# Assembling the 64-block inverses of two heads together, alternating in the array's groups

## The chip, the cores and the metric

The kernel runs on one core of a Trainium2 chip. The metric is the device time of one execution in microseconds; the median of three executions before the change is 1605.24 us (1601.2 to 1608.65). The core has five engines with queues of their own: TensorE (PE, whose weight loads the profile lists as PEld), VectorE (DVE), ScalarE (ACT), GpSimd (POOL) and SyncE (SP, which issues most of the transfers). TensorE's array is 128 x 128; a matmul with at most 32 rows and 32 columns of weights can be placed in one 32 x 32 tile of it (`tile_position=(row, column)`), and then reads operands from the partitions of its rows and writes PSUM partitions of its columns.

## The reference

One layer of a hybrid decoder on 512 prompt tokens and 32 sample tokens (8 sequences of 4): RMSNorm, one input projection, three parallel mixers that read it (RWKV-7 time mixing with 16 heads of 64, sparse attention with an indexer, cross-attention into 256 memory tokens), a gate on each, and an output projection with a final RMSNorm. The change touches the RWKV-7 part alone. Its recurrence over tokens, for each head, is

```python
def step(S, inp):
    r_t, k_t, v_t, w_t, kk_t, a_t = inp
    sa = jnp.einsum('bhvk,bhk->bhv', S, -kk_t)
    S = (S * w_t[:, :, None, :] + sa[..., None] * (kk_t * a_t)[:, :, None, :]
         + v_t[..., None] * k_t[:, :, None, :])
    return S, jnp.einsum('bhvk,bhk->bhv', S, r_t)
```

The kernel does not step through the tokens. It works on chunks of 64: inside a chunk the values `sa` solve a triangular system of 64 equations, whose matrix depends on the keys alone. So the inverse T of each chunk's matrix is made ahead, for all chunks at once, and then a loop over the 8 chunks carries the state.

## The kernel before, in words

After the norm the kernel runs the projections that attention needs, attention itself, and then `rwkv_group(g, ...)` for g = 0 to 3. One call, a head group, holds four heads: `j` (0, 1) is the pair, `h` (0, 1) the head in it, and a head's rows lie on partitions 64h to 64h + 63. Weights of every dense projection come as `raw` tiles of 128 x 512 by SP's queue, are split by ACT into a high part (L341, `wh`) and by DVE into the rest (L344, `wl`), and enter three float32r matmuls with 272 columns for each half of the tokens.

The order of the work is not written by hand. A planner takes every instruction with a priority and issues on each engine what is ready by its own estimate, the smaller number first; the kernel sets the priorities by `level(...)`. Matmuls of dense projections have level "fill", those of RWKV the normal one, so a dense matmul is issued where no RWKV matmul is ready. The projections for the next head group (`ahead("k")`, `ahead("v")`, `ahead("r")`) and the gates are the dense work beside a head group. On the chip each engine then executes its queue in the order planned.

Inside `rwkv_group`:

- L1198 to L1273: decays, keys and the products of keys in each chunk. `MBT` holds for each head and chunk the 64 x 64 matrix of products, of which the block from the first 32 tokens to the last 32 is used below.
- L1292 to L1298: DVE solves all 32 x 32 diagonal blocks of the triangular matrices together (64 blocks on 128 partitions), 31 steps of two operations.
- L1300 to L1302 and L1365 to L1373: the solved blocks go by DRAM (`vd`) into `TT`, the tile with T: partitions 64h + 32b hold the diagonal block b of head h. Two loads serve each head, the two of head 0 first.
- L1377 to L1393, the assembly: the block beside the diagonal is a product of three 32 x 32 matrices, for 16 (pair, chunk) combinations of each h. The loop over h takes one head after the other. DVE transposes the first diagonal block (L1381, one operation for each pair), 16 matmuls multiply it with the block of `MBT` (step 1, L1384), one ACT copy moves the 512 columns from PSUM (L1386), 16 matmuls multiply with the second diagonal block (step 2, L1389), and two ACT copies put the result into `TT` (L1392). Head h works in tile (64h, 64h + 32) of the array in step 1 and in (64h + 32, 64h) in step 2. Each step of each head has a PSUM bank of its own, from a ring of three (`"sc"` and `"tp"` share it).
- L1406 to L1470, `sample()`: the 32 sample tokens, in pieces between the chunks; its first matmuls are 64 x 64 with 8 columns.
- L1486 to L1534: the loop over the 8 chunks. Its products `p1` (L1500) don't need T; `pa` (L1512) does, four matmuls into one bank, `for j` outside and `for h` inside.

All matmuls of RWKV go through `mm`, so the profile gives them line 222, transposes by PE line 228. The tiles that lie in `slots` and `late` are told apart only by these names.

Of the kernel before, what the change touches and what calls it, by code (L numbers as in the profile page):

```python
# [124 lines left out]
def emit(ctx, tc, A):  # L125
    nc = tc.nc
    P = 128
# [14 lines left out]
    def R(shape, dt=F32, name="R", hot=False):  # L142
        n = math.prod(shape[1:]) * (2 if dt == BF16 else 4) // 4
        k = -(-n // SLOT)
        if k > 1:

            i = max((range(j, j + k) for j in range(0, NSLOT, k) if set(range(j, j + k)) <= set(free)),
                    key=lambda r: min(map(free.index, r)))
            for j in i:
                free.remove(j)  # L150
        else:
            i = (free.pop(-1 if hot else 0),)
        o = i[0] % 4 * SLOT
        t = quads[i[0] // 4][:shape[0], o:o + n]
        if dt != F32:
            t = t.bitcast(dt)
        if len(shape) > 2:
            ax = ["abcdefg"[d] for d in range(len(shape) - 1)]
            t = t.rearrange("p (%s) -> p %s" % (" ".join(ax), " ".join(ax)),
                            **{a: shape[d + 1] for d, a in enumerate(ax)})  # L160
        held[id(t)] = (i, t)
        return t

    def F(*ts):
        for t in ts:
            if isinstance(t, list):
                F(*t)
            else:
                free.extend(held.pop(id(t))[0])

    def S(shape, dt=F32, tag=None, bufs=None, name=None):
        return spool.tile(shape, dt, tag=tag, name=name or tag, bufs=bufs)

    def PS(shape, tag, dt=F32):
        tag, bufs = {"acc": ("acc", 3), "tp": ("ts", 3), "sc": ("ts", 3)}.get(tag, (tag, 1))
        return ppool.tile(shape, dt, tag=tag, name="ps_" + tag, bufs=bufs)

    act, dve, pool, pe = nc.scalar, nc.vector, nc.gpsimd, nc.tensor
# [5 lines left out]
    @contextmanager  # L184
    def level(n):
        old, tc.cur_priority = tc.cur_priority, levels[n]
        yield
        levels[n], tc.cur_priority = tc.cur_priority, old
# [31 lines left out]
    def mm(out, lhsT, rhs, start=True, stop=True, **kw):  # L220
        with level("fill") if in_side[0] else nullcontext():
            return pe.matmul(out, lhsT=lhsT, rhs=rhs, start=start, stop=stop, **kw)  # L222
# [115 lines left out]
    def split_w(raw, m):  # L338
        wh = wpool.tile([P, KG, P], F32R, tag="wh", name="wh", bufs=3)
        wl = wpool.tile([P, KG, P], F32R, tag="wl", name="wl", bufs=3)  # L340
        splits.append(act.activation(wh[:, :, :m], raw[:, :, :m], AF.Copy))  # L341
        lo_ctr[0] += 1
        eng = pool if lo_ctr[1] and lo_ctr[0] % lo_ctr[1] == 0 else dve
        eng.tensor_tensor(wl[:, :, :m], raw[:, :, :m], wh[:, :, :m].bitcast(F32), op=OP.subtract)  # L344
        return wh, wl
# [54 lines left out]
    for k in range(KO):  # L400
        raw = wpool.tile([P, KG, P], F32, tag="raw", name="raw", bufs=4)
        with level("top"):
# [3 lines left out]
            w = [flat2(t) for t in split_w(raw, P)]  # L406
# [22 lines left out]
    ok_, _ = VROWS["k_a"]  # L429
# [548 lines left out]
    for j in range(4):  # L978
        din(COL["va"] + j * P,
            lambda h, t0, t1, acc, j=j: act.activation(VT[j // 2][:, j % 2, t0:t1], acc[:, :t1 - t0], AF.Copy))  # L980
# [153 lines left out]
    for j in range(4):  # L1134
        din(COL["qm"] + j * P,
            lambda h, t0, t1, acc, j=j: act.activation(QM[j // 2][:, j % 2, t0:t1], acc[:, :t1 - t0], AF.Copy))
# [43 lines left out]
    def rwkv_group(g, pending, XK, XV, XR):  # L1180
# [3 lines left out]
        def ahead(nm, hot=False):  # L1184
            if g < 3:
                with level("late"):
                    nxt.append(rwkv_proj(g + 1, nm, hot))
# [10 lines left out]
        for j in range(2):  # L1198
# [4 lines left out]
            w = W2A2[:, j * P:(j + 1) * P]  # L1203
# [20 lines left out]
            for t0, t1_ in HV:  # L1224
                ps = PS([P, 512], "sc")
# [20 lines left out]
        MBT = R([P, 2, NCH, 64], name="mbt")  # L1246
        md = dpool.tile([64, 1024], F32, name="md", bufs=2)
        mds = dpool.tile([32, 16], F32, name="mds", bufs=2)
        for h in range(2):
            for j in range(2):  # L1250
                for q in range(2):
                    n0 = q * 4
                    ps = PS([P, 4, P], "sc")
# [14 lines left out]
        for h in range(2):  # L1268
            ps = PS([P, 512], "sc")
# [10 lines left out]
        for j in range(2):  # L1280
            dve.scalar_tensor_tensor(RK[:, j], XR[:, j], vec("r_k", 2 * g + j), XK[:, j], op0=OP.mult, op1=OP.mult)
            for (t0, t1), tag in zip(HV, "Lc"):
                ps = PS([P, 512], tag)
# [8 lines left out]
        for s_ in range(31):  # L1292
            i, w = s_ + 1, 31 - s_
            r = (i + 1) // 2
            t = S([P, 136], tag="tb", bufs=1)[:, :r * w].rearrange("p (i w) -> p i w", i=r)
# [18 lines left out]
        for s_ in range(3):  # L1314
            i, w = s_ + 1, 3 - s_
            t = S([32, 4], tag="tbs", bufs=1)[:, :i * w].rearrange("p (i w) -> p i w", i=i)
# [18 lines left out]
        for w in range(2):  # L1335
            p = PS([P, 2, 2, P], "tp")
# [9 lines left out]
        for j in range(2):  # L1346
            p = PS([P, 512], "tp")
# [7 lines left out]
        for j in range(2):  # L1355
            BKT.append(R([P, NCH, P], name="bkt", hot=j > 0))
            for q in range(2):
                p = PS([P, 512], "tp")
# [6 lines left out]
        TT = R([P, 2, NCH, 64], name="tt")  # L1365
        WG = R([P, 2, 512], name="wg")
# [7 lines left out]
        F(MB, VB, XV)  # L1374
        ahead("v")
        ahead("r")
        for h in range(2):  # L1377
            r0, r1 = 64 * h, 64 * h + 32
            w1 = WG[r0:r0 + 32, 0].rearrange("p (i t) -> p i t", t=32)
            for j in range(2):  # L1380
                dve.transpose(w1[:, j * 8:(j + 1) * 8], TT[r0:r0 + 32, j, :, 0:32])  # L1381
            ps = PS([P, 512], "sc")
            for i in range(16):
                mm(ps[r1:r1 + 32, i * 32:(i + 1) * 32], MBT[r0:r0 + 32, i // 8, i % 8, 32:64], w1[:, i],  # L1384
                   tile_position=(r0, r1))
            act.copy(WG[r1:r1 + 32, 1], ps[r1:r1 + 32])  # L1386
            ps = PS([P, 512], "sc")
            for i in range(16):
                mm(ps[r0:r0 + 32, i * 32:(i + 1) * 32], WG[r1:r1 + 32, 1, i * 32:(i + 1) * 32],  # L1389
                   TT[r1:r1 + 32, i // 8, i % 8, 32:64], tile_position=(r1, r0))  # L1390
            for j in range(2):
                act.copy(TT[r0:r0 + 32, j, :, 32:64],  # L1392
                         ps[r0:r0 + 32, j * 256:(j + 1) * 256].rearrange("p (n t) -> p n t", t=32))  # L1393
        F(WG, MBT)

        s0 = R([P, 2, NB, 64], name="smp")
# [88 lines left out]
        for n in range(NCH):  # L1485
            w, i = n // 4, n % 4  # L1486
# [10 lines left out]
            for u in range(2):  # L1497
                for j in range(2):
                    for h in range(2):
                        ins = mm(p1[HS[u], j, h], LB[j][h][:, c0 + 64 * u:c0 + 64 * u + 64], SV[w][:, i, j, h],  # L1500
                                 tile_position=(0, 64 * u))
# [20 lines left out]
            if n < NCH - 1:  # L1522
                w1, i1 = (n + 1) // 4, (n + 1) % 4
# [51 lines left out]
    for g in range(4):  # L1575
        pending, pr = rwkv_group(g, pending, *pr)
# [11 lines left out]
    for i in (4, 5, 6, 7, 0, 1, 2, 3):  # L1588
        if i not in YG:
            gated(i)  # L1590
        t, y = YT[i // 2][:, i % 2 * 2:i % 2 * 2 + 2], YG[i]
# [95 lines left out]
    for g in range(4):  # L1687
# [3 lines left out]
        for n, k in enumerate(KORD):  # L1691
# [3 lines left out]
            with level("fill"):  # L1695
# [5 lines left out]
                if n % 4 == 3:  # L1701

                    for j, (k, raw) in enumerate(raws):
                        mm(accs[4][32 * j:32 * j + 32], YS[:, k], raw, start=n == 3, stop=n == KO - 1,
                           tile_position=(0, 32 * j), skip_group_check=True)
# [74 lines left out]
```

## Time and profile before

| | before |
|---|---|
| median of 3 runs | 1605.24 us (1601.2 to 1608.65) |
| profiled execution | 1605.69 us, its span 1603.9 us |
| PE busy | 1517.4 us, 95% of the span |
| DVE busy | 946.7 us, 59% |
| ACT busy | 679.0 us, 42% |
| POOL busy | 309.2 us, 19% |
| mean granted TensorE clock | 0.98 of full speed |

The span goes from the first to the last instruction of the profiled execution. A busy PE is one with a matmul under way; matmuls overlap, so the busy time of a group is not the sum of its durations. Idle time of an engine is listed with what ended it. In timelines a line merges instructions of one kind that follow each other: the time of the first start, the time from there to the last end, and their number.

### The profile page before, as it was taken

What the parts mean: (1) busy time and instruction counts of PE and PEld (TensorE: products, weight loads), DVE (VectorE), ACT (ScalarE), POOL (GpSimd) and SP (SyncE); (2) the same over time, 40 slices, a digit from 0 to 9 for tenths busy, and PEclk for the clock granted to TensorE, in tenths of its full rate; (3) what the DMA queues carried; (4) which work ended last, traced back from release to release, by engine and by line L of the source; (5) the groups of instructions that cost most, each with busy time, mean ns of one, the idle gap of its engine ahead of it and who ended that gap; (6) DMA issues with size and microseconds to landing.
All of it is one profiled execution on the core that took longest, in us unless ns stands there. A gap on an engine that the chain in (4) does not pass through costs nothing.

```text
span 1603.9 us, 31129 instructions
## 1 busy us (share of the span) xinstructions
PE 1517.4 (95%) x11855; PEld 1292.9 (81%) x11855; DVE 946.7 (59%) x2697; ACT 679.0 (42%) x1482; POOL 309.2 (19%) x463
## 2 busy tenths in 40 slices
PE   8899999889989889889999999999999998999997
PEld 7799955889878875568898898799889988977775
DVE  5846677988565642115864893598368746623233
ACT  7656643222224423225633563465355444522223
POOL 0010121210454544320103011201310023001110
PEclk9999999999989999799999999999999999999999
DMA  7633232322697774456341243225123745472223
GB/s 279 201 109 80 73 113 60 94 69 72 208 292 222 226 213 127 125 173 195 95 113 48 59 115 72 57 60 150 45 57 91 188 145 160 147 232 79 92 93 138
DMA packets 227893, 207.12 MB, mean 129 GB/s; under 512 B 44768, under 2 KB 183200, under 8 KB 227232
## 3 DMA queue, kind: packets, MB, share of 16 engines
q1 hardware_dynamic: 214048, 158.99, 34.3%
q0 software_dynamic: 13696, 46.15, 9.2%
q8 instruction: 93, 1.52, 0.4%
q14 instruction: 56, 0.46, 0.1%
HBM read 180.89 MB, written 24.19 MB: 128 GB/s over the span
## 4 chain that ended last, share of the span: by engine, by line
PE 60%; issue 16%; DVE 11%; ACT 4%; DMA 4%; POOL 3%; another core or an unknown queue 1%; SPq 0%; POOLq 0%; DVEq 0%; ACTq 0%
PE ps_acc L222 31%; PE ps_ts L222 14%; PE ps_c L222 7%; PE ps_L L222 5%; DVE wl L344 2%; PE ps_ts L228 2%; POOL sw L477 2%; DMA late<-qd 1%; DVE slots L1150 1%; ACT wh L341 1%; DMA slots<-qd 1%; POOL wl L344 1%; DVE slots L904 1%; DVE late L785 1%
## 5 line engine op out<-in xcount | busy, mean ns | idle before, releaser
L222 PE MATMUL ps_acc<-xt,wh 128*128 128x272 f32 (+1 forms) x4224 | 862.7, 296 | 6.4 <-ACT lc L442 4.1
L222 PEld LDWEIGHTS ps_acc<-xt,wh 128*128 128x128 f32 (+1 forms) x4224 | 681.8, 190 | 30.1 <-issue 12.3
L222 PE MATMUL ps_acc<-xt,wl 128*128 128x272 f32 (+1 forms) x2112 | 625.4, 296 | 0.0
L222 PEld LDWEIGHTS ps_acc<-xt,wl 128*128 128x128 f32 (+1 forms) x2112 | 402.4, 191 | 9.0 <-issue 2.2
L341 ACT ACTIVATE wh<-raw 128x512 fp32r<-128x512 f32 (+1 forms) x296 | 185.1, 626 | 308.9 <-PE ps_acc L222 261.7
L344 DVE TENSOR_TENSOR wl<-raw,wh 128x512 fp32r<-128x512 f32 (+1 forms) x285 | 196.1, 691 | 133.6 <-ACT wh L341 117.6
L1684 DVE TENSOR_TENSOR wl<-raw,wh 128x512 fp32r<-128x512 f32 x58 | 42.8, 741 | 108.2 <-ACT wh L1683 99.8
L1683 ACT ACTIVATE wh<-raw 128x512 fp32r<-128x512 f32 x58 | 36.3, 630 | 115.4 <-PE ps_c L222 104.3
L222 PE MATMUL ps_acc<-wh,yt 128*128 128x512 f32 x192 | 61.5, 401 | 0.1
L222 PE MATMUL ps_ts<-wh,yt 128*128 128x512 f32 x156 | 50.3, 402 | 0.0
L477 POOL TENSOR_TENSOR sw<-sw,slots 128x272 f32<-128x272 f32 (+1 forms) x18 | 13.9, 773 | 185.2 <-ACT sw L475 185.2
L222 PEld LDWEIGHTS ps_acc<-wh,yt 128*128 128x128 f32 x192 | 35.4, 188 | 13.8 <-ACT wh L1683 5.9
L887 POOL DMA_INDIRECT slots<-ck,gix x36 | 37.4, 1040 | 38.0 <-DVE slots L904 24.0
L887 POOL DMA_INDIRECT slots<-cv,gix x32 | 30.5, 955 | 50.4 <-PE ps_L L222 28.5
L222 PEld LDWEIGHTS ps_ts<-wh,yt 128*128 128x128 f32 x156 | 28.7, 188 | 12.1 <-ACT wh L1683 5.0
L222 PE MATMUL ps_L<-late,slots 32*32 32x512 f32 (+3 forms) x192 | 38.3, 550 | 0.2 <-DMA late<-cmv 0.2
L222 PE MATMUL ps_ts<-slots,slots 64*64 64x512 f32 (+6 forms) x250 | 37.3, 322 | 0.2 <-DVE slots L1381 0.2
L222 PE MATMUL ps_acc<-wl,yt 128*128 128x512 f32 x96 | 37.4, 390 | 0.0
L887 POOL DMA_INDIRECT late<-cv,gix x32 | 30.3, 946 | 32.8 <-PE ps_L L222 23.5
L222 PE MATMUL ps_c<-wh,yt 128*128 128x512 f32 x116 | 36.5, 396 | 0.0
L544 DVE SCALAR_TENSOR_TENSOR slots<-tm,wtm,slots 128x256 f32<-128x256 f32 (+2 forms) x45 | 29.3, 656 | 10.3 <-ACT tm L540 9.7
L439 DVE SCALAR_TENSOR_TENSOR slots<-ps_acc,vecs,slots 128x271 f32<-128x271 f32 (+2 forms) x72 | 26.6, 397 | 13.6 <-ACT slots L438 12.7
(552 smaller groups left out, 2547.6 us busy)
## 6 DMA issues: line engine op xcount, KB each, us to landing
raw<-w_in SPq DMA_DIRECT2D x260, 256.0 KB
raw<-w_out SPq DMA_DIRECT2D x64, 256.0 KB
slots<-xT SPq DMA_DIRECT2D x4, 1088.0 KB
raw<-w_mk SPq DMA_DIRECT2D x16, 256.0 KB
raw<-w_mem SPq DMA_DIRECT2D x16, 256.0 KB
slots<-qd POOLq DMA_DIRECT2D x8, 512.0 KB
late<-qd POOLq DMA_DIRECT2D x8, 512.0 KB
slots<-xp SPq DMA_DIRECT2D x8, 512.0 KB
```

The costliest lines, as they stand in the source:

```text
L222: return pe.matmul(out, lhsT=lhsT, rhs=rhs, start=start, stop=stop, **kw)
L228: return pe.transpose(out, in_, T["ident"][b:b + k, b:b + k])
L341: splits.append(act.activation(wh[:, :, :m], raw[:, :, :m], AF.Copy))
L344: eng.tensor_tensor(wl[:, :, :m], raw[:, :, :m], wh[:, :, :m].bitcast(F32), op=OP.subtract)
L439: add = lambda o, prev: dve.scalar_tensor_tensor(o, prev, mu, o, op0=OP.mult, op1=OP.add)
L477: pool.tensor_tensor(sw[:np_], sw[:np_], sin[:np_, t0:t1], op=OP.mult)
L544: dve.scalar_tensor_tensor(SCP[i], rl[:, :nk], WTM[:, i, hd:hd + 1], SCP[i], op0=OP.mult, op1=OP.add)
L785: dve.tensor_scalar(oa[:, :, a], val[:, 1, sl].rearrange("p (n q) -> p n q", q=4), a, None, op0=OP.is_equal)
L887: pool.indirect_dma_start(out=dst[:, u], out_offset=None, in_=src, in_offset=bass.IndirectOffsetOnAxis(ap=GIX[:, 2 * q + u:2 * q + u + 1], ...
L904: ins = dve.scalar_tensor_tensor(kg[:, u, c], kg[:, u, c], 1.0, qb[:, c], op0=OP.mult, op1=OP.mult, accum_out=SCA[:, u, h, q:q + 1])
L1683: act.activation(wh, raw, AF.Copy)
L1684: dve.tensor_tensor(wl, raw, wh.bitcast(F32), op=OP.subtract)
```

## The change

The loop over h goes. The transposes of both heads come first, then all 32 matmuls of step 1, head 0 and head 1 in turn, into one PSUM bank, then a copy for each head, ACT for head 0 and DVE for head 1, then step 2 in the same way. The second copies take 512 columns in one operation where there were two of 256. The matmuls, their operands and the tiles of the array are the same; two PSUM banks are taken in each head group instead of four. The loads of `TT` and all that stands around are as before.

```diff
         F(MB, VB, XV)
         ahead("v")
         ahead("r")
-        for h in range(2):
-            r0, r1 = 64 * h, 64 * h + 32
-            w1 = WG[r0:r0 + 32, 0].rearrange("p (i t) -> p i t", t=32)
-            for j in range(2):
-                dve.transpose(w1[:, j * 8:(j + 1) * 8], TT[r0:r0 + 32, j, :, 0:32])
-            ps = PS([P, 512], "sc")
-            for i in range(16):
-                mm(ps[r1:r1 + 32, i * 32:(i + 1) * 32], MBT[r0:r0 + 32, i // 8, i % 8, 32:64], w1[:, i],
-                   tile_position=(r0, r1))
-            act.copy(WG[r1:r1 + 32, 1], ps[r1:r1 + 32])
-            ps = PS([P, 512], "sc")
-            for i in range(16):
-                mm(ps[r0:r0 + 32, i * 32:(i + 1) * 32], WG[r1:r1 + 32, 1, i * 32:(i + 1) * 32],
-                   TT[r1:r1 + 32, i // 8, i % 8, 32:64], tile_position=(r1, r0))
-            for j in range(2):
-                act.copy(TT[r0:r0 + 32, j, :, 32:64],
-                         ps[r0:r0 + 32, j * 256:(j + 1) * 256].rearrange("p (n t) -> p n t", t=32))
+        rows = [(slice(64 * h, 64 * h + 32), slice(64 * h + 32, 64 * h + 64)) for h in range(2)]
+        w1 = [WG[q0, 0].rearrange("p (i t) -> p i t", t=32) for q0, _ in rows]
+        for j in range(2):
+            for (q0, _), w in zip(rows, w1):
+                dve.transpose(w[:, j * 8:(j + 1) * 8], TT[q0, j, :, 0:32])
+        ps = PS([P, 512], "sc")
+        for i in range(16):
+            for (q0, q1), w in zip(rows, w1):
+                mm(ps[q1, i * 32:(i + 1) * 32], MBT[q0, i // 8, i % 8, 32:64], w[:, i],
+                   tile_position=(q0.start, q1.start))
+        for (_, q1), f in zip(rows, (act.copy, dve.tensor_copy)):
+            f(WG[q1, 1], ps[q1])
+        ps = PS([P, 512], "sc")
+        for i in range(16):
+            for q0, q1 in rows:
+                mm(ps[q0, i * 32:(i + 1) * 32], WG[q1, 1, i * 32:(i + 1) * 32], TT[q1, i // 8, i % 8, 32:64],
+                   tile_position=(q1.start, q0.start))
+        for (q0, _), f in zip(rows, (act.copy, dve.tensor_copy)):
+            f(TT[q0, :, :, 32:64], ps[q0].rearrange("p (j n t) -> p j n t", j=2, t=32))
         F(WG, MBT)
```

## Rows read from the trace of the kernel before

**Rows 1.** The page, parts 1 and 2: busy time of the engines, and TensorE's granted clock in 40 equal slices of the span, in tenths of full speed.

```profile
PE 1517.4 (95%) x11855; PEld 1292.9 (81%) x11855; DVE 946.7 (59%) x2697; ACT 679.0 (42%) x1482; POOL 309.2 (19%) x463
...
PEclk9999999999989999799999999999999999999999
```

**Rows 2.** The table of stretches for 820 to 880, 940 to 1000, 1120 to 1180 and 1240 to 1300 us, which hold the assemblies of head groups 0 to 3: its line of sums.

```profile
sum 240.00, PE 237.98 PEld 210.31 DVE 118.23 ACT 94.59 POOL 44.26; mean PE 59.50 PEld 52.58 DVE 29.56 ACT 23.65 POOL 11.06
```

**Rows 3.** What PE waited for from 800 to 1300 us: us in total, times, longest.

```profile
PE ps_ts L222 <- DVE late L1381: 0.7, 1, 0.7
PE ps_c L222 <- issue: 0.6, 1, 0.6
...
PE ps_ts L222 <- DVE slots L1381: 0.2, 1, 0.2
```

**Rows 4.** The timeline of PE in the assembly of head group 0: start, us from there to the last end, engine, line, operation, tiles, tile of the array, shape, number. 128x272 is dense work.

```profile
828.53 0.66 PE L222 MATMUL ps_ts<-slots,late 32*32 32x32 f32 x16
...
829.57 0.69 PE L222 MATMUL ps_ts<-slots,late 32*32 32x32 f32 x16
...
831.41 0.41 PE L222 MATMUL ps_acc<-xt,wh 128*128 128x272 f32 x2
831.75 1.19 PE L222 MATMUL ps_ts<-late,slots 32*32 32x32 f32 x32
832.87 0.39 PE L222 MATMUL ps_acc<-xt,wl 128*128 128x272 f32 x1
833.10 0.41 PE L222 MATMUL ps_acc<-xt,wh 128*128 128x272 f32 x2
...
833.57 0.33 PE L222 MATMUL ps_c<-bs,late 64*64 64x64 f32 x2
...
837.78 1.19 PE L222 MATMUL ps_ts<-late,slots 32*32 32x32 f32 x32
838.90 1.10 PE L222 MATMUL ps_ts<-slots,late 64*64 64x8 f32 x32
```

**Rows 5.** The timeline of the weight loads (PEld), two places with loads 64 columns wide: `p1` of chunk 1, four loads for one tile of the array, and `pa` of chunk 1, eight loads whose matmuls alternate between the tiles (0, 0) and (64, 64) and write one PSUM bank.

```profile
844.36 0.31 PEld L222 LDWEIGHTS ps_c<-slots,slots 128*64 128x64 f32 x4
...
846.89 0.31 PEld L222 LDWEIGHTS ps_c<-bs,late 64*64 64x64 f32 x8
```

**Rows 6.** The same view in an earlier stage (sample attention): the first and the last of four lines of weight loads, 32 columns wide, for four column tiles in turn.

```profile
415.53 0.11 PEld L222 LDWEIGHTS ps_ts<-late 128*32 128x32 f32 x2 [0.21 <-DVE keepbias L824]
...
415.57 0.12 PEld L222 LDWEIGHTS ps_ts<-late,slots 128*32 128x32 f32 x2
```

**Rows 7.** The groups of instructions by form, PE: the bf16 matmuls with 32 columns; number, busy us, mean ns of one, idle before.

```profile
L222 PE MATMUL ps_L<-slots,late 128*128 128x32 bf16 x256 | 6.8, 177 | 0.9 <-DVE late L785 0.8
```

**Rows 8.** The timeline of PE in head groups 1 and 2, at the first `pa` matmul, and what DVE waited for from 820 to 1350 us at its copy behind ACT's from the same bank (us, times, longest).

```profile
978.84 0.32 PE L222 MATMUL ps_c<-bs,slots 64*64 64x64 f32 x2
...
1126.13 0.33 PE L222 MATMUL ps_c<-bs,slots 64*64 64x64 f32 x2
...
DVE bs L1506 <- ACT bs L1505: 23.4, 17, 1.9
```

**Rows 9.** The timeline of DVE at the transposes of the assembly: for each head group the line of head 0 and the line of head 1; in brackets DVE's idle time before and what ended it.

```profile
827.96 0.75 DVE L1381 STREAM_TRANSPOSE slots<-late 32x256 f32<-32x256 f32 x2
...
833.13 0.76 DVE L1381 STREAM_TRANSPOSE slots<-late 32x256 f32<-32x256 f32 x2 [0.42 <-DMA late<-vd]
...
973.04 0.76 DVE L1381 STREAM_TRANSPOSE late<-slots 32x256 f32<-32x256 f32 x2 [0.27 <-DMA slots<-vd]
...
979.88 0.76 DVE L1381 STREAM_TRANSPOSE late<-slots 32x256 f32<-32x256 f32 x2
...
1120.51 0.76 DVE L1381 STREAM_TRANSPOSE slots<-slots 32x256 f32<-32x256 f32 x2
...
1125.30 0.76 DVE L1381 STREAM_TRANSPOSE slots<-slots 32x256 f32<-32x256 f32 x2
...
1278.90 0.43 DVE L1381 STREAM_TRANSPOSE late<-slots 32x256 f32<-32x256 f32 x1 [1.48 <-DMA slots<-vd]
...
1281.18 0.76 DVE L1381 STREAM_TRANSPOSE late<-slots 32x256 f32<-32x256 f32 x2 [0.92 <-DMA slots<-vd]
```

**Rows 10.** The views of single lines: number, shortest/median/longest ns of one, first and last start, shape.

```profile
L1386 ACT COPY slots<-ps_ts x4: 577/578/580, 830.3 to 1129.5; 32x512 f32<-32x512 f32 x4
...
L1392 ACT COPY slots<-ps_ts x12: 357/360/363, 978.2 to 1289.7; 32x256 f32<-32x256 f32 x12
...
L1260 DVE TENSOR_TENSOR late<-ps_ts,cmain x14: 693/694/696, 911.3 to 1231.6; 64x512 f32<-64x512 f32 x14
```

**Rows 11.** The table of stretches behind the assemblies of head groups 1 and 2 (us of the stretch; busy us and instructions of PE, PEld, DVE, ACT and POOL; granted clock; DMA share; GB/s), and the timeline of PE in it.

```profile
984.00:988.00 4.00, 4.00 (x65) 3.23 (x62) 0.39 (x2) 0.63 (x2) 1.04 (x1) 0.68 0.23 63
988.00:992.00 4.00, 4.00 (x22) 3.38 (x23) 0.70 (x3) 0.70 (x3) 1.31 (x4) 0.50 0.00 0
...
1134.00:1138.00 4.00, 4.00 (x21) 3.19 (x22) 0.41 (x2) 0.53 (x2) 0.00 (x0) 0.50 0.16 46
...
988.12 0.43 PE L222 MATMUL ps_acc<-xt,wl 128*128 128x272 f32 x1
988.35 0.65 PE L222 MATMUL ps_acc<-xt,wh 128*128 128x272 f32 x2
988.80 0.43 PE L222 MATMUL ps_acc<-xt,wl 128*128 128x272 f32 x1
```

## The prediction

> **What bounds the kernel now.** I read the page first: TensorE (PE) is busy for 95% of the span at a granted clock of 9 tenths or more in nearly every slice [rows 1]. An average over stages says little about one stage, so next the table of stretches: over the four stretches of 60 us that hold the four assemblies PE is busy for 237.98 of 240 us [rows 2], and in all of 800 to 1300 us it waited 0.9 us for the transposes that feed the assembly and 0.6 us for nothing visible [rows 3]. So the dense projections of the next head group fill every gap between the small matmuls, and the price of the assembly is not its chain of waits but the PE time that it takes from the dense work. The reader is to see that in the timeline of the first assembly [rows 4]: dense matmuls (128x272), a block of 32x32 ones, dense ones again, without holes.
>
> From rows 4 come the two prices. (a) Each float32 matmul leaves two records; a head has 16 + 16 + 32 of them, so a head group has 128 and the kernel 512. A block of 32 lasts 1.19 us, one of 16 0.69 us: 0.50/16 = 31 ns a record, all in one tile of the array. I use 32 ns. (b) Dense matmuls start 0.12 us apart (two in 0.41 us, the second of 0.29). The block of 32 at 831.75 stands between a dense start at 831.53 (831.41 + 0.12) and the second dense start after it at 833.10: 1.57 us, less two dense steps (0.25) and 32 records (1.0), leaves about 0.3 us. That is the fee for changing the shape of the tiles and back. A head group has six blocks; the last runs straight into the sample state's 64x8 matmuls (837.78 and 838.90) and pays about 0.07. So PE spends now 512 x 0.032 + 20 x 0.3 + 4 x 0.07 = 16.4 + 6.3 = 22.7 us.
>
> **The change, part by part.**
>
> *Alternating matmuls.* The number of matmuls stays; consecutive ones now lie in different row and column groups. No 32x32 pair like it is in the trace. The nearest rows are 64-wide: four weight loads in one tile take 0.31 us, eight that alternate between two tiles, with the results in one PSUM bank, take the same 0.31 us [rows 5]. So two tiles take their loads side by side, and a record costs half. Four column tiles with loads 32 wide start eight of them within 0.05 us [rows 6], so loads of this width overlap too. Bounds: 7 ns a record (rows 6, with four tiles) to 32 ns (no overlap); an alternating row dearer than its one-tile counterpart I did not find. I take 16 ns: 512 x 0.016 = 8.2 us less.
>
> The Trainium skill, TensorEngine Tiling (Array Packing), "Gotcha 1: PSUM Pressure", says that different row tiles cannot use one PSUM bank at the same time, which is what this change does (rows 0 and 64, one bank); by that rule these 8.2 us would be 0. The eight loads at 846.89 do the same in one bank, with rows 0 and 64, and they overlap, so the trace speaks against it.
>
> *Fewer blocks.* Does the order of the code survive the planner, which issues what is ready? The first head's data is there earlier: its transposes come 5.2, 6.8, 4.8 and 2.3 us before the second's [rows 9]. Matmuls to one bank keep their written order: after the first head's half of T was copied, only one 64x64 matmul (two records) ran at 833.57 [rows 4], and the same at 978.84 and 1126.13 [rows 8]; the next one of that head waited for the other head's. So I expect in each head group a lone matmul (2 records), a block of 62, after the copies again a lone one, and a block of 62: four blocks instead of six, 16 in all, four of them next to the sample's. 12 x 0.3 + 4 x 0.07 = 3.9 against 6.3: 2.4 us less. Between 8 blocks (3.6 us less) and 24 (0) lie the ends.
>
> *Copies.* In each head group ACT loses 0.58 + 0.72 us (one 32x512 copy and two of 32x256), DVE gains two copies of 512 columns from PSUM; no row shows that copy, the nearest is 64x512 at 0.69 us [rows 10]. The second copy is queued behind the first, because two engines read one bank in turn (DVE waited 23.4 us for ACT at L1506 [rows 8]). From the first step 1 matmul of a head pair to the last copy I get 1.0 + 0.1 + 0.58 + 0.69 + 0.1 + 1.0 + 0.1 + 0.58 + 0.69 = 4.8 us; counted in the same way the second head alone takes 0.69 + 0.69 + 0.1 + 0.58 + 0.1 + 1.19 + 0.1 + 0.72 = 4.2 us now. The chunk loop behind it starts some 0.6 us later, which costs nothing while dense work fills PE, and 4 x 0.6 = 2.4 us if that cover were gone. What queues behind the waiting DVE copy is the split of the next weight tile (L344); three buffers of it, 24 dense matmuls or 3 us each, stand ahead. Range: 0 to 2.4 us; I take 0.
>
> *The wait for the second head.* Step 1 now ends only with the later load. PE executes in a fixed order, so where a load lands later than planned PE stands still. Today it does that for 0.7 and 0.2 us [rows 3], mostly for the first head; the second head had slack. DVE waited 0.42 and 0.92 us for second heads' loads [rows 9]. I take 0.25 us a head group, 1.0 us in all; the ends are 0 and the whole gap between the heads, 19.1 us.
>
> *The clock.* Directly behind two of the four assemblies, after 32x32 and 64x8 matmuls, the granted clock fell to 0.50 (1.2 GHz): 0.68 over 984 to 988 and 0.50 over 988 to 992 make 2.6 + 4.0 = 6.6 us at that level, and 1134 to 1138 shows the same [rows 11]. There three dense starts take 0.68 us (988.12 to 988.80), 0.227 us each instead of 0.125: 6.6 us lose 6.6 x (1 - 0.125/0.227) = 3.0 us. The change halves the time in which PE does only small matmuls, and puts dense ones between the two long blocks. I count one of the two falls as gone, 3.0 us; the ends are 6.0 gained and 3.0 lost (a third one).
>
> **Sum.** 8.2 + 2.4 - 1.0 + 3.0 = 12.6 us. The profiled execution took 1605.69 us (span 1603.9), 0.45 above the median of the runs; 1605.7 - 12.6 = 1593.1. Forecast 1593, with its own range 1588 to 1598 (both falls or none, and some 2 us for the planner's other choices).
>
> **Rivals.**
>
> *A limit on the rate of records.* The pairs overlap, but PE can't start records that fast for 62 in a row. For: the quickest long run of matmuls that I found, 256 in bf16, needs 6.8/256 = 26.6 ns each [rows 7], and no row holds 16 ns for long. Against: the short burst of rows 6. Gain 512 x (32 - 26.6) = 2.8 instead of 8.2: 1593.1 + 5.4 = 1598.5.
> The Trainium skill, TensorE: Matmul & The Clock Gate, "Wait — 56ns, not 53.3ns?", gives such a floor, about 25 ns from start to start, and by it the time would be some 1597.7 (an estimate). Starts 7 ns apart, as rows 6 imply, contradict it for a burst, not for a long block.
>
> *No overlap, or the planner runs the heads one after the other.* Then only blocks are saved or not even these, the clock behaves as now, and the stall stays: gain 2.4 - 1.0 down to -1.0: 1604.3 to 1606.7. For: the heads' loads are far apart. Against: rows 4, 5 and 8.
>
> *Slower: PE stands still for the second head.* If the planner puts the block of 62 where the first head is ready, PE, which works in order, waits out the gap of each head group, 5.2 + 6.8 + 4.8 + 2.3 = 19.1 us [rows 9] instead of 1.0; and both falls of the clock stay as they are, so that the 3.0 us are not gained: 1593.1 + 18.1 + 3.0 = 1614.2. It decides from 12.6 + 1.0 - 3.0 = 10.6 us of such waits, over half of the gaps. For: the longer wait for one bank. Against: today's plan already knows when the second head comes and fills that gap with dense work.
>
> *Better than forecast.* Both falls of the clock and every stall go: 1588 or less.
>
> **How the numbers follow.** A difference under 0.5%, 8.0 us, can't be told from none for this kernel; faster means below 1597.2. Forecast 0.59 (nine tenths of its own range is below that: 0.53), rate limit 0.19 (a third below: 0.06), no overlap 0.12, slower 0.06, better 0.04. Faster 0.53 + 0.06 + 0.04 = 0.63, same 0.31, slower 0.06. The range from 1587 to 1603 leaves out most of no overlap and slower, and little below.
>
> **What would show it.** In the changed kernel's timeline: blocks of about 62 records (32x32) lasting 1.1 to 1.2 us with two starts close together, lone blocks of 2 before them, one DVE copy of 32x512 right behind ACT's; the sum of small blocks and fees near 12 us instead of 22.7; dense matmuls without holes around them. A pitch of 25 or more in the long blocks makes the rate limit true; blocks of 16 make the planner's rival true; PE waiting for L1381's transposes for over 1 us makes the slower one true. A clock that still falls behind two assemblies takes 3 us from the gain. What makes the whole prediction wrong is a plan so different that PE loses time far from the assembly.

## The result, and the profile after

The changed kernel takes 1593.22 us (median of 20 executions, 1581.25 to 1604.33) against 1606.49 us of the kernel before in 20 executions beside it: ratio 0.9923 [0.9902, 0.9944]. The forecast was 1593, inside a range of 1587 to 1603.

The profiled execution took 1597.6 us. Parts 1 and 2 of its page, the lines that answer to [rows 1]:

```profile
span 1595.8 us, 31111 instructions
...
PE 1507.9 (94%) x11855; PEld 1285.4 (81%) x11855; DVE 957.5 (60%) x2705; ACT 675.6 (42%) x1466; POOL 309.5 (19%) x463
...
PEclk9999999999989999799799999999999999999999
```

The number of matmuls is the same, PE is busy for 9.5 us less, and the clock line has a dip in a new place.

The timeline of PE in the assembly of head group 0, in the columns of [rows 4]:

```profile
834.92 0.29 PE L222 MATMUL ps_acc<-xt,wh 128*128 128x272 f32 x1
835.27 0.22 PE L222 MATMUL ps_ts<-slots,late 32*32 32x32 f32 x2
835.42 0.39 PE L222 MATMUL ps_acc<-xt,wh 128*128 128x272 f32 x1
...
840.16 0.29 PE L222 MATMUL ps_acc<-xt,wl 128*128 128x272 f32 x1
840.38 1.19 PE L222 MATMUL ps_ts<-slots,late 32*32 32x32 f32 x62
841.50 0.52 PE L222 MATMUL ps_acc<-xt,wh 128*128 128x272 f32 x2
...
842.45 0.24 PE L222 MATMUL ps_ts<-late,slots 32*32 32x32 f32 x2
842.63 1.10 PE L222 MATMUL ps_ts<-slots,late 64*64 64x8 f32 x32
843.66 0.52 PE L222 MATMUL ps_acc<-xt,wh 128*128 128x272 f32 x2
...
844.61 1.19 PE L222 MATMUL ps_ts<-late,slots 32*32 32x32 f32 x62
845.73 0.52 PE L222 MATMUL ps_acc<-xt,wh 128*128 128x272 f32 x2
```

The reader is to see three things. A block of 62 lasts as long as a block of 32 did. Beside the block of 2 it gives (1.19 - 0.24) / 60 = 15.8 ns for a record, where one tile took (1.19 - 0.24) / 30 = 31.7 in the blocks of 32 before. And the head group runs as 2, 62, 2, 62: the matmul of head 0 alone, far ahead, then everything else. The other three head groups show the same four blocks.

The price of the assembly can be taken from such timelines: for each block the time from the last dense start before it to the second dense start after it, less two usual steps between dense starts (0.125 us each); where a block runs straight into another small matmul, to the start of that one, less one step. Over all blocks of 32x32 this is 24.6 us before (24 blocks) and 15.8 us after (16 blocks). I call it the PE cost below. Stalls are in it, and so is what a block loses where the clock falls during it, so that two profiles of one kernel can differ: the changed one has 15.8 here and 17.3 in set 1.

What PE waited for from 800 to 1300 us (total, times, longest), which answers to [rows 3], and the one stall in the timeline of head group 3:

```profile
PE ps_ts L222 <- DVE late L1381: 2.5, 1, 2.5
PE ps_acc L222 <- ACT lc L442: 0.9, 1, 0.9
PE ps_c L222 <- DVE slots L1529: 0.7, 1, 0.7
```

```profile
1275.19 0.29 PE L222 MATMUL ps_acc<-xt,wl 128*128 128x272 f32 x1
1277.97 0.22 PE L222 MATMUL ps_ts<-late,late 32*32 32x32 f32 x2 [2.49 <-DVE late L1381]
1278.11 0.52 PE L222 MATMUL ps_acc<-xt,wh 128*128 128x272 f32 x2
```

The stalled block is the lone one of two records, the first matmul of head 0. It waits for the first transpose of head 0, and that for head 0's load, as the timeline of DVE shows:

```profile
1277.39 0.43 DVE L1381 STREAM_TRANSPOSE late<-slots 32x256 f32<-32x256 f32 x1 [2.67 <-DMA slots<-vd]
```

So in the four assemblies' stretches PE stands idle for 5.7 us, where it was 2.0 before [rows 2]; the stall is 2.5 us of it:

```profile
sum 240.00, PE 234.33 PEld 211.93 DVE 135.78 ACT 90.61 POOL 40.16; mean PE 58.58 PEld 52.98 DVE 33.95 ACT 22.65 POOL 10.04
```

The granted clock, in the table of stretches with the columns of [rows 11]: 784 to 788 lies ahead of the first assembly, the next two behind the assemblies of head groups 1 and 2, the last behind the stall.

```profile
784.00:788.00 4.00, 4.00 (x16) 3.54 (x17) 1.85 (x4) 1.95 (x7) 0.00 (x0) 0.50 0.01 4
992.00:996.00 4.00, 4.00 (x60) 3.37 (x54) 0.97 (x2) 1.20 (x4) 0.00 (x0) 1.00 0.23 62
1136.00:1140.00 4.00, 4.00 (x49) 3.38 (x42) 1.94 (x7) 2.34 (x7) 0.00 (x0) 1.00 0.01 4
1278.00:1282.00 4.00, 4.00 (x21) 3.96 (x22) 1.63 (x4) 2.19 (x4) 0.00 (x0) 0.57 0.22 41
```

Both falls of [rows 11] are gone from this execution, but between 720 and 1340 us two others are there: one of 17 us (776.8 to 793.9) at 1.2 GHz where the change does nothing (the profile of the kernel before in set 1 has one as long in the same place, 58 us ahead of the first assembly), and one of 3.4 us behind the stall. Where the clock falls differs from execution to execution, and the time follows: of the 20 executions one with a mean granted clock of 0.987 took 1581.25 us, one with 0.972 took 1603.24.

**Reading at equal clock.** Each execution has its time and its mean granted clock. For each set of kernels that shared one chip I laid parallel lines through time against clock, one for each kernel with one slope for all, and read them at 0.985. In the first set the slope was 1.45 us (error 0.09) for 0.001 of mean clock, in the second 1.44 (0.09), in the third, with the fewest executions, 1.13 (0.15). The distance between two lines is what a kernel saves with the clock taken out; the rest of its gain came with the clock. Such differences carry an error of 0.8 to 1.4 us. Two executions of set 1 that took 2790.74 and 3653.25 us are left out of the ratios and lines.

### The profile page after: what moved, and what is told of

It reads as the page before. It is cut to its first block, busy times and chain, and to the rows that moved or that the text cites. A ratio compares the mean times of both kernels' runs of the same rounds, so it can differ in the third digit from the quotient of the medians.

```text
span 1595.8 us, 31111 instructions
## 1 busy us (share of the span) xinstructions
PE 1507.9 (94%) x11855; PEld 1285.4 (81%) x11855; DVE 957.5 (60%) x2705; ACT 675.6 (42%) x1466; POOL 309.5 (19%) x463
## 4 chain that ended last, share of the span: by engine, by line
PE 59%; issue 16%; DVE 11%; DMA 6%; ACT 4%; POOL 3%; another core or an unknown queue 1%; SPq 0%; DVEq 0%; POOLq 0%; ACTq 0%
PE ps_acc L222 30%; PE ps_ts L222 14%; PE ps_c L222 7%; PE ps_L L222 5%; DVE wl L344 3%; DMA late<-qd 2%; PE ps_ts L228 2%; POOL sw L477 2%; DMA slots<-gd 1%; ACT wh L341 1%; DVE late L904 1%; POOL wl L344 1%; DVE slots L904 1%; DVE late L785 1%
## 5 line engine op out<-in xcount | busy, mean ns | idle before, releaser
L344 DVE TENSOR_TENSOR wl<-raw,wh 128x512 fp32r<-128x512 f32 (+1 forms) x285 | 203.7, 718 | 121.9 <-ACT wh L341 113.0
L438 ACT ACTIVATE slots<-ps_acc,omu 128x272 f32<-128x272 f32 x48 | 23.3, 488 | 31.2 <-PE ps_acc L222 29.5
```

Of the source, the lines that this page charges most:

```text
L438: act.activation(dst[:, t0:t1], acc[:, :n], AF.Copy, scale=om)
```

## The experiments

**Set 1: is it the alternation, and does the bank matter?** Four kernels on one chip; the kernel before, as the common partner, took 1579.12 us there (mean clock 0.984). The first is the kernel before itself, unmodified.

> The kernel before, run again for the granted clock of each of its executions. Theory (the gain is PE time: records of 16 ns instead of 32, and 16 blocks instead of 24): at an equal mean clock the changed kernel is 8 to 11 us shorter, and the mean clock of the two is about the same. Rival (the gain is fewer falls of the clock): at an equal clock the two take the same time within 2 us, and the changed kernel's mean clock is higher by some 0.007.

Measured: 1579.46 us, ratio 0.999 [0.9964, 1.0016]. A difference of 0.3% is within what this measurement can't tell from none.

The second is the changed kernel, unmodified.

> The changed kernel again, on the same chip as the others of this set: 0.990 to 0.994 of the time before. In its trace four blocks of 2, 62, 2 and 62 records in each head group, 16.4 ns a record.

Measured: 1567.33 us, ratio 0.9912 [0.9883, 0.9941]. At equal clock it saves 7.6 us (error 0.9), a little less than the 8 to 11 expected, and its mean clock is not, as that theory had it, about the same as before. The means of the executions differ by 13.6 us; the remaining 6.0 go with the clock, whose mean is 0.0042 higher (4.2 x 1.45 = 6.1). Its profile still has a fall of the clock at the assemblies of head groups 1 and 2 (10.2 and 6.8 us long, the first from before the last long block on), so one trace does not show what the clock gave over many executions. The PE cost is 17.3 us, with that slowed block in it, and the stall of head group 3 is there again (2.7 us).

The third keeps the merged loops, the one bank and the copies, and takes the alternation away: all 16 of head 0, then all 16 of head 1.

```diff
-        for i in range(16):
-            for (q0, q1), w in zip(rows, w1):
+        for (q0, q1), w in zip(rows, w1):
+            for i in range(16):
...
-        for i in range(16):
-            for q0, q1 in rows:
+        for q0, q1 in rows:
+            for i in range(16):
```

> The changed kernel, but in each step all 16 matmuls of head 0 and then all 16 of head 1, still in one bank and with the same copies. Theory: 31 to 32 ns a record again, 512 x 16 = 8 us given back, and as the planner runs head 0 when it is ready, four to six blocks a head group: 0.997 to 1.002 of the time before. Rival (bank, copies or the clock made the gain, not the alternation): 0.990 to 0.994 as in the changed kernel.

Measured: 1584.2 us, ratio 1.0013 [0.998, 1.0046]; at equal clock 0.4 us above the kernel before, PE cost 25.5 us. Its timeline of PE in one head group:

```profile
961.03 0.66 PE L222 MATMUL ps_ts<-late 32*32 32x32 f32 x16 [0.48 <-DVE late L1381]
...
962.07 0.69 PE L222 MATMUL ps_ts<-late 32*32 32x32 f32 x16
...
966.27 0.69 PE L222 MATMUL ps_ts<-late 32*32 32x32 f32 x16
...
967.83 0.69 PE L222 MATMUL ps_ts<-late 32*32 32x32 f32 x16
...
969.39 2.11 PE L222 MATMUL ps_ts<-slots,late 32*32 32x32 f32 x64
```

Blocks of 16 in 0.69 us and of 64 in 2.11 us: (2.11 - 0.69) / 48 = 30 ns a record, 32 ns from start to start but for a few records that overlap where the two heads meet. Merging the heads without alternating is worth nothing that this measurement can see.

The fourth alternates as the change does, but each head has a PSUM bank of its own in each step.

```diff
-        ps = PS([P, 512], "sc")
+        ps = [PS([P, 512], "sc") for _ in rows]
...
-            for (q0, q1), w in zip(rows, w1):
-                mm(ps[q1, i * 32:(i + 1) * 32], ...
+            for (q0, q1), w, b in zip(rows, w1, ps):
+                mm(b[q1, i * 32:(i + 1) * 32], ...
...
```

> The changed kernel, written in alternation as there, but each head has a PSUM bank of its own in each step. Theory: without the one bank nothing keeps the written order, head 0 runs alone when its load is there, the records take 31 to 32 ns again and there are five or six blocks a head group: 0.998 to 1.003 of the time before. Rival (the alternation as written is enough, or one bank slows the pairs): 0.988 to 0.994.

Measured: 1581.2 us, ratio 0.9995 [0.9967, 1.0022]; at equal clock 2.2 us saved, PE cost 21.5 us. Its timeline, head 0's first step and a later block of one head:

```profile
812.42 0.66 PE L222 MATMUL ps_ts<-slots,late 32*32 32x32 f32 x16
...
813.45 0.69 PE L222 MATMUL ps_ts<-slots,late 32*32 32x32 f32 x16
...
822.06 1.19 PE L222 MATMUL ps_ts<-late,slots 32*32 32x32 f32 x32
```

With two banks the planner sends all of head 0 as soon as it is ready. The alternation that the code asks for does not reach PE; only where a block of one head runs into the other's do some records alternate, up to some twenty in a block of 64. The one bank is what keeps the written order. The 2.2 us left fit the number of blocks, 17 instead of 24 (7 x 0.3 = 2.1, an estimate).

**Set 2: the copies, the lone block, and more tiles.** Another chip, with the kernel before at 1613.67 us (mean clock 0.975). First, all copies on ACT instead of one of each pair on DVE:

```diff
-        for (_, q1), f in zip(rows, (act.copy, dve.tensor_copy)):
+        for (_, q1), f in zip(rows, (act.copy, act.copy)):
...
-        for (q0, _), f in zip(rows, (act.copy, dve.tensor_copy)):
+        for (q0, _), f in zip(rows, (act.copy, act.copy)):
```

> The changed kernel with all four copies of a head group on ACT, none on DVE. Theory: the copies lie under dense work, wherever they run: at an equal clock within 1.5 us of the changed kernel, 0.989 to 0.994 of the time before. Rival (relief of ACT, whose copies delay the split of weights, is part of the gain): 3 us or more longer than the changed kernel.

Measured: 1602.18 us, ratio 0.9937 [0.9905, 0.9969]; 9.1 us saved at equal clock (error 0.8), PE cost 17.1. That is near the changed kernel's 7.6 (error 0.9), which was taken on another chip, and it is not the 3 us less that the rival gave. So the engine of the copies has no part in the gain that this measurement can see.

Second, head 1 goes first in each pair of matmuls. Head 1's load is the later one, so nothing can run ahead of it in the bank's order:

```diff
-            for (q0, q1), w in zip(rows, w1):
+            for (q0, q1), w in ((rows[1], w1[1]), (rows[0], w1[0])):
...
-            for q0, q1 in rows:
+            for q0, q1 in rows[::-1]:
```

> The changed kernel with head 1 ahead of head 0 in each pair of matmuls, so that the first matmul of a step is the one whose data comes last. Theory (fees for changing the tiles are paid per block, and a lone early matmul makes PE wait for head 0's load): no lone blocks of 2, eight blocks in all; eight fees of 0.15 to 0.4 us and the wait of some 2.5 us in head group 3 go, so at an equal clock 3 to 5 us less than the changed kernel, 10 to 13 less than before. Rival (PE then waits as long for head 1): within 1 us of the changed kernel.

Measured: 1588.25 us, ratio 0.9841 [0.9793, 0.9889]; 14.6 us saved at equal clock (error 1.2; 10 to 13 were expected), PE cost 11.3 us in 9 blocks. Its timeline and its wait for the transposes:

```profile
842.19 1.20 PE L222 MATMUL ps_ts<-slots,late 32*32 32x32 f32 x64
...
845.40 1.20 PE L222 MATMUL ps_ts<-late,slots 32*32 32x32 f32 x64
```

```profile
PE ps_ts L222 <- DVE late L1381: 0.5, 1, 0.5
```

The lone blocks are gone with their fees, and the stall is down from 2.5 to 0.5 us. The PE cost is 5.8 us below that of the version with copies on ACT, 0.5 us of it a wait inside one of that version's long blocks; the time at equal clock is 5.5 us below (error 1.2). So the lone blocks, fees and stall together, are worth some 5 us.

Third, the two pairs `j` get different column groups, so that four tiles of the array alternate (each copy is cut in two, since the halves lie on different partitions):

```diff
+        for n in range(NCH):
+            for j in range(2):
+                for (q0, q1), w in zip(rows, w1):
+                    d = q0 if j else q1
+                    mm(ps[d, n * 32:(n + 1) * 32], MBT[q0, j, n, 32:64], w[:, j * 8 + n],
+                       tile_position=(q0.start, d.start))
+        for (q0, q1), f in zip(rows, (act.copy, dve.tensor_copy)):
+            for j in range(2):
+                f(WG[q1, 1, j * 256:(j + 1) * 256], ps[q0 if j else q1, :256])
...
```

> The changed kernel, but the two pairs of a head take different column groups as well, so that four tiles of the array alternate; each step then has four copies of 256 columns instead of two of 512. Theory (a record costs its tile 32 ns, tiles run side by side): 8 ns a record, blocks of 58 to 62 in 0.5 us instead of 1.0, so 4 us less PE time than the changed kernel, 0.987 to 0.991 of the time before. Rival (PE can't start records in a long block faster than one in some 16 ns, or 25): the block stays at 1.0 us, or 1.5, and the time that of the changed kernel.

Measured: 1601.41 us, ratio 0.9924 [0.9897, 0.995]; 10.6 us saved at equal clock (error 0.8). The timeline has now three blocks in each step, 24 in all:

```profile
834.20 0.22 PE L222 MATMUL ps_ts<-slots,late 32*32 32x32 f32 x2
...
839.31 0.25 PE L222 MATMUL ps_ts<-slots,late 32*32 32x32 f32 x4
...
839.94 0.70 PE L222 MATMUL ps_ts<-slots,late 32*32 32x32 f32 x58
```

A record costs (0.70 - 0.25) / 54 = 8.3 ns: half of 15.8, so no limit at 16 or at 26 ns stands in the way. But more blocks eat it (PE cost 16.7 us against 17.1 with copies on ACT), so the 4 us expected did not come, and the granted clock is 0.50 directly behind the first three assemblies:

```profile
845.00:849.00 4.00, 4.00 (x19) 2.89 (x18) 1.54 (x3) 0.95 (x2) 0.00 (x0) 0.50 0.00 0
995.00:999.00 4.00, 4.00 (x19) 2.90 (x18) 0.86 (x3) 0.35 (x1) 0.00 (x0) 0.50 0.01 4
1142.00:1146.00 4.00, 4.00 (x19) 2.92 (x17) 2.19 (x7) 1.50 (x4) 0.00 (x0) 0.50 0.01 4
```

**Set 3: four tiles and the late head first, and the better version again.** A third chip, with the kernel before at 1604.48 us (mean clock 0.977). The first kernel joins the last two: `for j in (1, 0)` and head 1 ahead of head 0 in both steps of the four-tile version.

> x_four with the order of its matmuls turned round as in x_late: head 1 ahead of head 0 and pair 1 ahead of pair 0, so that each step's first matmul needs the data that comes last. Theory (records on four tiles at 9 ns, a fee per block): eight blocks of 64 in 0.55 us, 6 to 7 us of PE time in all against 11.3 in x_late and some 16 to 17 in the changed kernel; at an equal clock 4 to 5 us less than x_late. Rival (four copies in turn and later loads eat it up): the time of x_late within 1.5 us.

Measured: 1592.64 us, ratio 0.9922 [0.9893, 0.9951]; 13.1 us saved at equal clock (error 1.1), PE cost 9.4 us in 8 blocks of 64, where 6 to 7 were expected. Its blocks are short (0.75 and 0.85 us in the lines below), but PE waits for the transposes here too, 1.6 us in head group 3, although head 1 goes first:

```profile
834.49 0.75 PE L222 MATMUL ps_ts<-slots,late 32*32 32x32 f32 x64
...
837.02 0.85 PE L222 MATMUL ps_ts<-late,slots 32*32 32x32 f32 x64
```

```profile
PE ps_ts L222 <- DVE late L1381: 1.6, 1, 1.6
```

The second is the two-tile version with head 1 first, once more.

> x_late again beside x_best, for an interval from more executions: at an equal clock 11 to 15 us less than before, 0.984 to 0.992 of its time. Rival (its first figure, from six executions, was the clock's): 0.992 or more, and less than 9 us at an equal clock.

Measured: 1584.32 us, ratio 0.9873 [0.9845, 0.9902]; 14.3 us saved at equal clock (error 1.3). What was expected of four tiles failed: at equal clock they are not 4 to 5 us cheaper but within 1.5 us of two, as the rival had it. Which of the two is ahead at equal clock can't be told: the difference of 1.2 us has an error of 1.4, and with the slope of the first set it is 0.4 us the other way. The two-tile version is the better one by its medians, 8.3 us, most of which goes with the clock (mean 0.982 against 0.977). The table of stretches behind the first assembly, first with four tiles, then with two:

```profile
840.00:844.00 4.00, 4.00 (x19) 3.26 (x19) 1.07 (x3) 1.16 (x3) 0.05 (x1) 0.50 0.25 66
```

```profile
838.00:842.00 4.00, 4.00 (x47) 3.54 (x46) 1.89 (x4) 1.25 (x4) 1.04 (x1) 1.00 0.00 0
```

Both four-tile versions show this fall behind each of their first three assemblies, and the first of them two more at its fourth, behind its stall and ahead of its last block. The two-tile version with head 1 first shows none in its profile of set 2 and one in that of set 3, of some 3.5 us (0.69 over 984 to 988 us, 0.88 over 988 to 992). With two tiles and head 0 first it stands at three of twelve assemblies (none in the profile after but the one behind the stall, two in the second profile of that kernel, one with the copies on ACT), in the two profiles of the kernel before at four of eight. That four tiles bring the fall is an association over these few profiles; why was not tried, and neither was why the PE cost of 9.4 us, 2 us below that of two tiles, does not show in the time. Both stay open.

## Why the prediction was right

*Alternating matmuls* (8.2 us less). Right: 512 x (31.7 - 15.8) = 8.1 us with the pitch of the blocks of 32 before and of 62 after. Without alternation the pitch within a head is back at 32 ns and the whole gain is gone; that run shows what the rows named in the prediction could not, as they set loads of 128 rows beside loads of 64. The limit on the rate of records is refuted, at 26.6 ns by the blocks of 62 and at 16 by those of 58. The Trainium skill, TensorEngine Tiling (Array Packing), "Gotcha 1: PSUM Pressure", says that different row tiles cannot use one PSUM bank at the same time; this use contradicts it, as rows 0 and 64 write one bank from different column groups and overlap, at 15.8 ns a record. The Trainium skill, TensorE: Matmul & The Clock Gate, "Wait — 56ns, not 53.3ns?", gives a floor of about 25 ns from start to start; across tiles 15.8 and 8.3 ns contradict it, in one tile, at 32 ns, nothing here does.

*Fewer blocks* (2.4 us less). Right in form: 2, 62, 2, 62 in every head group, 16 in all. The fees come to 15.8 - 2.5 (stall) - 512 x 0.0158 = 5.2 us against 3.9 predicted; counted alike, the kernel before has 24.6 - 0.9 - 512 x 0.0317 = 7.5 against 6.3, so 2.3 us went. Without the stalls the PE cost is 13.3 us instead of 23.7, where the prediction's sign was 12 instead of 22.7. The detail that differs: the sample's matmuls now follow the lone block of step 2, and the last long block pays its full fee. The reason given, that one bank keeps the written order, is what the two-bank version shows.

*Copies* (0). Right: with all of them on ACT the gain is the same within the errors. (ACT loses 1.44 us a head group and not 1.30, since its two copies of 256 columns become one of 512, too.) DVE's copies waited behind ACT's and took what the nearest row said (0.70 us, and the second step's the same):

```profile
842.22 0.70 DVE L1388 COPY slots<-ps_ts 32x512 f32<-32x512 f32 x1 [0.34 <-ACT slots L1388]
...
846.45 0.69 DVE L1395 COPY late<-ps_ts 32x512 f32<-32x512 f32 x1 [2.45 <-ACT late L1395]
```

*The wait for the second head* (1.0 us more). The size is near, 2.5 against 0.9 us before, 1.6 more, but the place is wrong. No second head was waited for longer: it is the lone matmul of head 0, issued early, that stood in PE's order ahead of its load in head group 3. It is there in all four profiles in which the alternation arrives with head 0 first, at 2.2 to 2.7 us. Putting head 1 first takes away that block and 2 us of the wait with two tiles, 0.7 us with four. The prediction named the lone block and charged it a fee; it did not see that a block sent as early as possible is the one most exposed to a late load.

*The clock* (3.0 us less). The mechanism as put, one of two falls gone, is not what the profiled execution shows. It lost both and got two others, and its mean clock is 0.978 where that of before was 0.980. Over many executions the clock's part was about 6 us in set 1 and, for the version with copies on ACT, some 2 us in set 2 (clock 0.0015 higher). Both lie within the ends stated, 6.0 gained to 3.0 lost, but 3.0 was an even guess between them and not a term that the runs confirm. Falls at the assemblies are two and two in the profiles of the kernel before, and none, two and one in those with two tiles and head 0 first, the one behind the stall not counted: on the mean one less, as put, but five profiles are too few to show it.

So the PE part was 8.2 + 2.4 - 1.0 = 9.6 predicted; the two traces give 24.6 - 15.8 = 8.8, and the lines at equal clock 7.6. The median's 13.3 us includes the clock's share, which on that chip can't be taken out, as the clock of the executions before is on record for the profiled one alone. That 12.6 came so close is in part luck: the PE part came 0.8 to 2.0 us short of its 9.6, and a share of the clock that was only guessed made up for it.

Of the rivals, heads one after the other is what the two-bank and the unalternated version do, and there the time is near that of before, as that rival priced it. In the changed kernel none gave the time. But by the prediction's own sign, PE waiting for L1381's transposes for over 1 us, the slower rival would have come true, with 2.5 us. The sign was badly set: that rival priced 19.1 us of waits for head 1, what came was 2.5 us for head 0, and the gain of 8.1 us outweighed it.

## What to carry to other kernels

Small matmuls that fill one tile of the array each cost half when neighbours in the queue lie in different row and column groups; where a planner orders the queue, look in the timeline whether the alternation arrived, and use one PSUM bank to hold it. Put the matmul whose data comes last first in such a group: one that can go early makes a block of its own, pays the fee, and stalls the engine when its load is late (here some 5 of 14.6 us). Where the granted clock differs from execution to execution, list time against clock before crediting a change with a difference of a few us.

## What the runs showed of the hardware that was not expected

Matmuls in four tiles of the array started 8.3 ns apart in a block of 58, half of what two tiles need and a quarter of one tile's 32. And the granted clock fell to 1.2 GHz behind the first three assemblies of both four-tile versions, where the blocks of 64 on two tiles, with the same work in 1.20 instead of 0.70 to 0.85 us, were followed by 2.4 GHz in seven of eight assemblies over two profiles. Why is not shown.
